# A decoder layer's RWKV mixer in units of two head pairs by 256 tokens, not one pair by 512

## The chip, the cores and the metric

The kernel runs on one core of a Trainium2 chip. The metric is the time of one execution in microseconds (us); "before" is the median of three runs. The profile is of one more execution of the same kernel.

## What is computed

One layer of a decoder for 1024 prompt tokens and 8 sample tokens (1032 columns, held as three pieces of 344 or as four of 256, the last with the 8 samples on top): a SwiGLU FFN, a token mixer, cross-attention into 256 memory tokens, a second FFN, each with a residual and a layer norm. The mixer is what the change touches:

```python
proj = h @ P['w_in']                       # RWKV columns, LRU columns, gates
...
def step(S, inp):                          # per head: 64 x 64 state S
    r_t, w_t, k_t, v_t, kk_t, a_t = inp
    sa = jnp.einsum('bhvk,bhk->bhv', S, -kk_t)
    S = S * w_t[:, :, None, :] + sa[..., None] * (kk_t * a_t)[:, :, None, :] + v_t[..., None] * k_t[:, :, None, :]
    y = jnp.einsum('bhvk,bhk->bhv', S, r_t)
    return S, y
...
_, hs = lax.associative_scan(_lin_combine, (a_t, b_t), axis=1)      # RG-LRU
merged = gates[:, :, 0] * rwkv_out + gates[:, :, 1] * lru_out
out = merged @ P['w_mix_out']
...
mk = (mem_prompt @ xa_wk[l]) ; mv = (mem_prompt @ xa_wv[l])         # attention's memory
```

There are 16 heads of 64 channels, held as 8 pairs of 128 partitions. The 8 samples take one step of the same recurrence from a given state.

## The kernel before

Matrix products keep fp32 accuracy by three products each (`mm3`, L125 to L127): the weight's high part times the input's high and low part (`wh` with HH, HL), and its low part `wl` with HH. Below such a product is called a gemm, and a gemm matmul of the mixer has 344 columns. A weight arrives in halves of 128x512: `split_half` loads one into a tile `raw` (L94, a DMA that SP issues), ScalarE (ACT) rounds it to `wh` (L99), VectorE (DVE) makes `wl` from `raw` and `wh` (L100), and only then is `raw` free. How many `raw` tiles and pairs of `wh`, `wl` there are is set by `more_weights`; in the mixer there is one `raw` and three of the others.

The mixer's recurrence goes in chunks of 64 tokens, in 16 units. Unit t is pair p = t//2 and half u = t%2: one pair by 512 tokens, 8 chunks. For a unit there is `stage` (elementwise work and the matrices within a chunk, SC, BK, AR, QZ), `inverse` (the inverse of the chunks' triangular matrices, on DVE and through DRAM, which ends with the PE group `m<-TB` at L932), and `chain` (the walk over the chunks). A chunk of `chain` has three dependent hops: `ch<-QZ,SC` (L1051), copied by DVE to `wsb` (L1053); `ch<-wsb,TT` (L1057), copied to QZ by DVE (L1063) for one head and by ACT for the other; `y<-QZ,BK` (L1067), scaled by DVE into the next chunk's QZ (L549). After four chunks a `post` makes the group norm and the gates of 256 tokens. `branch` is the RG-LRU; `samples_a`, `samples_b`, `samples_c` are the samples of a pair. In `samples_b` each row of a small DRAM tile T is broadcast by DMA into a tile `row` (L1115) and DVE combines it with the states. `project`, called by `gemms`, does the input projection.

The loop over the units runs `rounds(26, streams, ...)`: in each of 26 rounds each stream (the chain of the unit before, the inverse, the stage of the next unit, branches, samples, gemms) takes its share of steps. That is the order of the program; a list scheduler then fixes, when the kernel is built, the order on every engine, and on the chip each engine runs its list from top to bottom. A DMA that SP is to issue stands in SP's list too.

In the last two units the gemms are those of `out_proj`, the product with w_mix. Behind the loop, `actx.close()` frees the mixer's buffers, `more_weights(S, ctx, 2, 1)` makes it three `raw` and four hl tiles, and the tail begins: the last chain, `out_last` (the last part of w_mix's product, onto `acc<-HD`, the residual), the layer norm, and `memory_kv`, which multiplies the memory by wk and wv: 32 halves, 384 matmuls (`kv<-memh,wh` and the like). Then come the queries and the first scores of attention, `s<-kvh,qh`.

Of the kernel before, what the change touches and what calls it, by code (L numbers as in the profile page):

```python
# [10 lines left out]
F32 = mybir.dt.float32  # L11
# [523 lines left out]

LATE = ("ev", "ref", "dend", "scl", "sm", "wsb", "sf", "ysb", "gsq", "ivc", "bv", "lm")


def mixer(octx, S, I, O, MG, HD, pre):
# [13 lines left out]
    with ExitStack() as ctx:  # L553
# [98 lines left out]
        def gemms(p):  # L652

            for q, xs, early in ((p + 1, tiles(p + 1)[:3], True), (p, tiles(p)[3 + (p == 0):], False)):
                if q < S.npairs:
                    for x in xs:
                        yield from project(q, *x, load_split(S, I["w_in"][x[0]]), CH3, psg, t1)
                    ends(q, early)


        with ExitStack() as c2:
# [78 lines left out]
        stages = itertools.cycle([st0] * 2 + [actx.enter_context(tc.tile_pool(name="msa", bufs=4))] * 4)  # L740
# [6 lines left out]
        def inv_norm(sq, ob, c, op, q, r, tag):  # L747
# [9 lines left out]
            yield  # L757
# [7 lines left out]
        def stage(p, n, P):  # L765

            col = lambda t: t[:, p:p + 1]
            c0, w = NCW[n]
            st = next(stages)
# [9 lines left out]
            for i in range(3):  # L779
                x = tmp("x%d" % i)[:, :w]  # L780
                mt = 8 * i + p
                ACT(x, R[:, i, 1:1 + w], scale=omu[:, mt:mt + 1])
                STT(x[:, 0:256], R[:, i, 0:256], mu[:, mt:mt + 1], x[:, 0:256], ALU.mult, ALU.add)
# [13 lines left out]
            if n == 3:  # L797
                P.sv = t1.tile([128, 6, 8], F32, tag="sv", name="sv", bufs=2)
                P.sg = t1.tile([128, 3, 8], F32, tag="sg", name="sg", bufs=2)
# [13 lines left out]
            bv = tmp("bv", 264, 6)[:, :w]  # L813
            TTo(bv, xv, pb, ALU.mult)
# [4 lines left out]
            ref, dend = P.ref, P.dend  # L819
# [6 lines left out]
            if n == 3:  # L826
# [3 lines left out]
                nc.vector.tensor_copy(out=P.sg[:, 0, :], in_=bv[:, 256:264])  # L830
# [15 lines left out]
            SC, BK = [], []  # L846
            QZ = st.tile([128, 4, 2, 64], F32, tag="QZ", name="QZ")
# [6 lines left out]
            for h in range(2):  # L854
                sc = st.tile([128, 4, 128], F32, tag="SC%d" % h, name="SC%d" % h)
                TTo(sc, q[h], mask.unsqueeze(1).to_broadcast([128, 4, 128]), ALU.mult)
                for b in range(2):
                    r0 = 64 * h + 32 * b
                    nc.sync.dma_start(out=P.D1[n // 2][b, h, 4 * (n % 2):4 * (n % 2) + 4].rearrange("c s t -> s c t"),
                                      in_=sc[r0:r0 + 32, :, 32 * b:32 * b + 32])  # L860
                ACT(P.L21[n // 2][64 * h:64 * h + 32, 4 * (n % 2):4 * (n % 2) + 4, :], sc[64 * h:64 * h + 32, :, 32:64])
# [20 lines left out]
            P.AR.append(AR)  # L882
            P.SC.append(SC)
            P.BK.append(BK)
            P.QZ.append(QZ)

        def inverse(p, u, P):

            TT = TTs[u]

            iv = ta.tile([128, 32, 32], F32, tag="iv", name="iv")
            for q in range(4):
                nc.sync.dma_start(out=iv[32 * q:32 * q + 32], in_=P.D1[u].rearrange("b h c s t -> (b h c) s t"))
# [27 lines left out]
            for h in range(2):  # L921
                B0 = slice(64 * h, 64 * h + 32)
                nc.vector.transpose(out=TN[B0], in_=TT[B0, :, 0:32])
                for c in range(0, 8, 2):
                    nc.tensor.matmul(q[half[h], c // 2, :], P.L21[u][B0, c:c + 2, :].rearrange("p c t -> p (c t)"),
# [12 lines left out]
            for n in (2 * u, 2 * u + 1):  # L938
                for h in range(2):
                    ACT(P.SC[n][h][half[h], :, 0:64], P.AR[n][half[h], :, 0, :])  # L940

        def branch(p, n, P):

            col = lambda t: t[:, p:p + 1]
            c0, w = NCW[n]
            if n == 0:
                P.wg = ta.tile([128, 2, 128], F32, tag="wg", name="wg")
# [17 lines left out]
            gr, gi, th = tmp("gr")[:, :w], tmp("gi")[:, :w], tmp("th")[:, :w]  # L965
# [14 lines left out]
            hs = tmp("lm", 264, 3)  # L980
# [3 lines left out]
            P.hl = tmp("hl", 9, 2)  # L984
# [19 lines left out]

        def post(p, n, P, Y):

            col = lambda t: t[:, p:p + 1]
            c0 = NCW[n][0]
# [3 lines left out]
            ACT(ysb, Y[:, 0:256])  # L1012
            yield
            q = Y[:, 256:512]
            nc.tensor.matmul(q, ones64, ysb, start=True, stop=True)
            TTo(ysb, ysb, q, ALU.subtract)
            ACT(sq, ysb, AF.Square)
            yield
            rs = yield from inv_norm(sq, ob64, GN_EPS, ALU.add, Y[:, 0:4], lambda: Y[:, 256:512], "ivc")
# [9 lines left out]
            if p < S.npairs - 1:  # L1029
                nc.sync.dma_start(out=MG[p, :, 256 * n:256 * n + 256], in_=ysb)  # L1030
            else:
                direct(p, 256 * n, 256, ysb)

        def chain(p, u, P):

            col = lambda t: t[:, p:p + 1]
            TT = TTs[u]
            U8 = slice(8 * u, 8 * u + 8)
            scl = tmp("scl", 8, 2)
            TTo(scl, P.dend[:, U8], P.ref[:, 8 * u + 1:8 * u + 9], ALU.add)  # L1040
            ACT(scl, scl, AF.Exp, scale=-C0)
            for c in range(8 * u, 8 * u + 8):
                n, cc = divmod(c, 4)
                c8 = c - 8 * u
                QZ, SC, BK, AR = P.QZ[n], P.SC[n], P.BK[n], P.AR[n]
                if cc == 0:
                    Y = pst("y", 512, 2)
                    Yc = Y[:, 0:256].rearrange("p (c t) -> p c t", t=64)
                pw, pz = psc(64), Y[:, 256 + 64 * cc:320 + 64 * cc]
                for h in range(2):  # L1050
                    nc.tensor.matmul(pw[half[h]], SC[h][:, cc, 0:64], QZ[:, cc, h, :], start=True, stop=True)  # L1051
                wsb = tmp("wsb", 64, 2)
                nc.vector.tensor_copy(out=wsb, in_=pw)  # L1053
                yield
                pu = psc(64)
                for h in range(2):
                    nc.tensor.matmul(pu[half[h]], TT[half[h], c8, :], wsb[half[h]], start=True, stop=True)  # L1057
                for h in range(2):
                    nc.tensor.matmul(Yc[half[h], cc, :], QZ[half[h], cc, h, :], AR[half[h], cc, 1, :], start=True,
                                     stop=False)  # L1060
                for h in range(2):
                    nc.tensor.matmul(pz[half[h]], ident[half[h], half[h]], QZ[half[h], cc, h, :], start=False, stop=False)
                nc.vector.tensor_copy(out=QZ[half[0], cc, 0, :], in_=pu[half[0]])  # L1063
                ACT(QZ[half[1], cc, 1, :], pu[half[1]])
                yield
                for h in range(2):
                    nc.tensor.matmul(pz[half[h]], BK[h][:, cc, :], QZ[:, cc, h, :], start=False, stop=False)  # L1067
                for h in range(2):
                    nc.tensor.matmul(Yc[half[h], cc, :], QZ[:, cc, h, :], SC[h][:, cc, 64:128], start=False,
                                     stop=True)  # L1070
                if c == 15:
                    sf = tmp("sf", 64)
                dst = [sf[half[h]] if c == 15 else P.QZ[(c + 1) // 4][half[h], (c + 1) % 4, h, :] for h in range(2)]
                for h in range(2):
                    TSC(dst[h], pz[half[h]], scl[half[h], c8:c8 + 1], None, ALU.mult, None)
                yield
                if cc == 3:
                    yield post(p, n, P, Y), 8
            if u == 1:
                nc.sync.dma_start(out=O["prwkv"][p], in_=sf)  # L1080

        def samples_a(p, P):
# [3 lines left out]
            v = tmp("v8", 8, 2, t1)  # L1086
# [11 lines left out]
            s = tmp("sT", 128, 1, t1)[0:40]  # L1098
# [4 lines left out]
        def samples_b(p, P):  # L1103

            y, T3 = tmp("y8", 8, 2, t1), P.T3
            P.y8 = y
            sv = P.sv
            b8 = lambda t: t.unsqueeze(2).to_broadcast([128, 8, 64])
            s_, t_ = (ta.tile([128, 8, 64], F32, tag=x, name=x) for x in ("ws", "wt"))
            nc.sync.dma_start(out=s_, in_=I["srwkv"][p].rearrange("p (b k) -> p b k", k=64))  # L1110

            def row(j):
                t = ta.tile([128, 8, 64], F32, tag="row", name="row", bufs=1)
                for h in range(2):
                    nc.sync.dma_start(out=t[half[h]], in_=T3[8 * j:8 * j + 8, 64 * h:64 * h + 64].unsqueeze(  # L1115
                        0).to_broadcast([64, 8, 64]))
                return t

            yield
            TTo(t_, s_, row(3), ALU.mult)  # L1120
# [534 lines left out]
```

## Time and profile before

| | us |
|---|---|
| runs | 3216.65, 3216.25, 3211.92; median 3216.25 |
| profiled execution | 3214.64, of which span 3212.9 |
| FFN 1 | 0 to about 740 |
| first projections and unit 0's stage and inverse | to 934.5 (end of the first inverse) |
| mixer's rounds | to 2019.9 (start of the last matmul of the last inverse) |
| tail of the mixer, memory's keys and values, queries | to 2181.3 (first scores) |
| attention and FFN 2 | to 3212.9 |

A PE record is a matmul pass: a matmul of 64 columns in fp32 leaves two. "idle before" is the time in which an engine stood still just before a group, with the one that released it. Records such as `x4` are several of one kind in a row. The granted clock is 1.00 when TensorE runs at full speed.

### The profile page before, as it was taken

To read this page: it belongs to the slowest core of one execution; us is meant where nothing else is said; L and a number is where in the kernel's file an instruction comes from. 1 tells how busy PE (TensorE), PEld (TensorE's weight loads), DVE (VectorE), ACT (ScalarE), POOL (GpSimd) and SP (SyncE) were. 2 spreads that over 40 slices of the span, in tenths; PEclk is the share of its full clock that TensorE was granted. 3 is DMA by queue.
4 is the path that set the end of the run, shared out by engine and by line. 5 is a ranking of instruction groups with operands and counts; after the bars stand their busy time and mean duration, and the time that the engine had idled before them with its cause. 6 is when DMAs were issued, how large, how long until landed. Compare 5 with 4: busy or idle time off the path is not lost. (4 is left out here: it accounts for less than half of the span.)

```text
span 3212.9 us, 63092 instructions
## 1 busy us (share of the span) xinstructions
PE 3068.3 (95%) x23312; PEld 2857.1 (89%) x23312; DVE 2247.5 (70%) x6072; ACT 1458.9 (45%) x3259; POOL 565.0 (18%) x526
## 2 busy tenths in 40 slices
PE   8999999999899999999999999889897999999997
PEld 8999999998798888887888878778887999999997
DVE  7666665574578887777888777666667666666556
ACT  5333352125546565656566665364235433334112
POOL 2222200132000101011010010250005322220111
PEclk9999999999999999999999989999999999999998
DMA  4222253314644444444444454654433222225321
GB/s 139 80 78 80 80 159 106 112 47 140 198 122 128 120 119 120 119 131 116 129 119 125 119 145 121 187 161 134 144 117 117 78 80 80 80 80 158 106 86 53
DMA packets 361078, 370.73 MB, mean 115 GB/s; under 512 B 141728, under 2 KB 259904, under 8 KB 360768
## 3 DMA queue, kind: packets, MB, share of 16 engines
q1 hardware_dynamic: 360768, 366.69, 38.3%
q8 instruction: 183, 3.00, 0.4%
q14 instruction: 127, 1.04, 0.1%
HBM read 269.42 MB, written 97.37 MB: 114 GB/s over the span
## 5 line engine op out<-in xcount | busy, mean ns | idle before, releaser
L125 PE MATMUL ps<-HH,wh 128*128 128x258 f32 (+1 forms) x2384 | 719.6, 302 | 17.2 <-ACT HH L508 7.5
L126 PE MATMUL ps<-HL,wh 128*128 128x258 f32 (+1 forms) x2384 | 717.8, 301 | 0.1
L127 PE MATMUL ps<-HH,wl 128*128 128x258 f32 (+1 forms) x2384 | 716.8, 301 | 0.0
L125 PE MATMUL g<-HH,wh 128*128 128x344 f32 (+2 forms) x1840 | 632.3, 344 | 18.5 <-ACT wh L99 5.9
L126 PE MATMUL g<-HL,wh 128*128 128x344 f32 (+2 forms) x1840 | 592.6, 323 | 0.9 <-POOL HL L215 0.8
L127 PE MATMUL g<-HH,wl 128*128 128x344 f32 (+2 forms) x1840 | 589.6, 323 | 0.5 <-DVE hl L991 0.2
L125 PEld LDWEIGHTS ps<-HH,wh 128*128 128x128 f32 x2384 | 452.4, 190 | 19.3 <-ACT HH L508 7.5
L126 PEld LDWEIGHTS ps<-HL,wh 128*128 128x128 f32 x2384 | 452.0, 190 | 0.6 <-DVE HL L509 0.5
L127 PEld LDWEIGHTS ps<-HH,wl 128*128 128x128 f32 x2384 | 451.3, 189 | 0.0
L125 PEld LDWEIGHTS g<-HH,wh 128*128 128x128 f32 x1840 | 354.4, 193 | 45.7 <-ACT wh L99 8.8
L126 PEld LDWEIGHTS g<-HL,wh 128*128 128x128 f32 x1840 | 355.3, 193 | 5.9 <-POOL HL L215 1.5
L127 PEld LDWEIGHTS g<-HH,wl 128*128 128x128 f32 x1840 | 353.0, 192 | 6.6 <-DVE wl L100 1.8
L228 ACT ACTIVATE wh<-raw 128x512 fp32r<-128x512 f32 x280 | 176.5, 631 | 322.0 <-PE ps L126 264.9
L334 POOL TENSOR_TENSOR raw<-raw 128x512 f32<-128x512 f32 x160 | 214.1, 1338 | 566.4 <-DVE wl L229 359.7
L229 DVE TENSOR_TENSOR wl<-raw,wh 128x512 fp32r<-128x512 f32 x280 | 205.3, 734 | 139.0 <-ACT wh L228 132.1
L100 DVE TENSOR_TENSOR wl<-raw,wh 128x512 fp32r<-128x512 f32 x301 | 218.6, 733 | 97.7 <-ACT wh L99 96.1
L99 ACT ACTIVATE wh<-raw 128x512 fp32r<-128x512 f32 x301 | 185.1, 626 | 217.8 <-PE ps L126 75.2
L442 DVE SCALAR_TENSOR_TENSOR acc<-ps,acc 128x344 f32<-128x344 f32 x336 | 168.4, 512 | 141.2 <-PE ps L127 140.6
L546 DVE TENSOR_TENSOR pr<-tq,iv 128x2 f32<-128x2 f32 (+30 forms) x496 | 162.3, 327 | 4.9 <-DVE iv L894 0.3
L551 ACT ACTIVATE ev<-g 128x344 f32<-128x344 f32 x192 | 87.3, 455 | 98.0 <-PE g L127 84.7
L754 POOL TENSOR_TENSOR ivc<-ivc,mhalf 128x4 f32<-128x4 f32 x32 | 34.9, 1090 | 526.4 <-DVE ivc L549 478.9
L551 ACT ACT_TABLE_LOAD x96 | 123.2, 1283 | 5.8 <-DMA raw<-in_w_in_dram 2.0
(417 smaller groups left out, 6570.5 us busy)
## 6 DMA issues: line engine op xcount, KB each, us to landing
raw<-in_wi_dram SPq DMA_DIRECT2D x176, 256.0 KB, 2.9
raw<-in_w_in_dram SPq DMA_DIRECT2D x116, 256.0 KB, 3.0
GD<-ev SPq DMA_DIRECT2D x168, 172.0 KB, 2.0
raw<-in_wo_dram SPq DMA_DIRECT2D x104, 256.0 KB, 3.1
raw<-HID SPq DMA_DIRECT2D x88, 258.0 KB, 3.2
HID<-g SPq DMA_DIRECT2D x80, 258.0 KB, 2.2
row<-T SPq DMA_DIRECT2D x80, 128.0 KB, 3.0
GD<-t SPq DMA_DIRECT2D x24, 344.0 KB, 4.0
```

The lines of the kernel that those rows point to most:

```text
L99: nc.scalar.activation(out=hi, in_=raw, func=AF.Identity)
L100: nc.vector.tensor_tensor(out=lo, in0=raw, in1=hi.bitcast(F32), op=ALU.subtract)
L125: nc.tensor.matmul(ps, wh, xh, start=first, stop=False)
L126: nc.tensor.matmul(ps, wh, xl, start=False, stop=False)
L127: nc.tensor.matmul(ps, wl, xh, start=False, stop=last)
L228: nc.scalar.activation(out=hi, in_=x, func=AF.Identity)
L229: nc.vector.tensor_tensor(out=lo, in0=x, in1=hi.bitcast(F32), op=ALU.subtract)
L334: pool_tt = lambda o, a, b, op: nc.gpsimd.tensor_tensor(out=o, in0=a, in1=b, op=op)
L442: nc.vector.scalar_tensor_tensor(out=a, in0=q, scalar=0.5 / ALPHA, in1=a, op0=ALU.mult, op1=ALU.add)
L546: TTo = lambda o, a, b, op: nc.vector.tensor_tensor(out=o, in0=a, in1=b, op=op)
L551: ACT = lambda o, a, f=AF.Identity, **kw: nc.scalar.activation(out=o, in_=a, func=f, **kw)
L754: nc.gpsimd.tensor_tensor(out=v, in0=v, in1=mhalf[:, 0:4], op=ALU.pow)
```

## The change

A unit is a group of two pairs by 256 tokens: group g = t//4, quarter n = t%4, still 16 units, each 4 chunks of 4 heads. So there are 64 chunk steps, each with the matmuls of two steps before. The three products of a step share one PSUM tile `ch`; the copies to `wsb` (now 128x128) and QZ (64x2x64) serve both pairs, and the scaling is a `TENSOR_TENSOR` with a broadcast factor. The loop has 13 rounds a unit. The gemms are one continuous stream, of which unit t takes FILL[t] steps; unit 0's stage is woven with 42 of them, and `rest` projects four tiles ahead of the rounds where it did two. Two posts follow a unit, one behind the other. `samples_b` runs both pairs of a group, one after the other, each in two halves of four samples, and loads its rows into the work tile `wt` itself, so that a load waits for the last use of `wt` and the next DVE step for the load. `out_proj` leaves out two pairs for all eight m, and `out_last` adds both for all of them. In the tail `more_weights(S, ctx, 2, 1)` is gone: the one `raw` and three hl tiles of the mixer stay.

```diff
 # rest(), ahead of the mixer's rounds
-                for x in tiles(0)[2:4]:
-                    yield from project(0, *x, load_split(S, I["w_in"][x[0]]), CH3, psl, lp)
-                ends(0, True)
+                for p, i in ((0, 2), (1, 0), (1, 1), (1, 2)):
+                    x = tiles(p)[i]
+                    yield from project(p, *x, load_split(S, I["w_in"][x[0]]), CH3, psl, lp)
...
-            weave((low_out(), 29), (rest(), 17))
+            weave((low_out(), 29), (rest(), 49))
...
 # post
-            ACT(ysb, Y[:, 0:256])
+            ACT(ysb, Y)
...
-            if p < S.npairs - 1:
+            if p < S.npairs - 2:
                 nc.sync.dma_start(out=MG[p, :, 256 * n:256 * n + 256], in_=ysb)
...
 # chain
-            for c in range(8 * u, 8 * u + 8):
...
-                pw, pz = psc(64), Y[:, 256 + 64 * cc:320 + 64 * cc]
+            for c in range(4):
...
+                ch = psc(384).rearrange("p (x i t) -> p x i t", i=2, t=64)
+                pw, pu, pz = (ch[:, x] for x in range(3))
+                for i, h in both:
+                    nc.tensor.matmul(pw[half[h], i], SC[i][h][:, c, 0:64], QZ[:, i, c, h, :], start=i == 0, stop=i == 1)
+                wsb = tmp("wsb", 128, 2).rearrange("p (i t) -> p i t", t=64)
+                nc.vector.tensor_copy(out=wsb, in_=pw)
+                yield
+                for i, h in both:
+                    nc.tensor.matmul(pu[half[h], i], TT[half[h], 4 * i + c, :], wsb[half[h], i], start=i == 0, stop=i == 1)
+                for i, h in both:
+                    nc.tensor.matmul(Yc[half[h], i, c, :], QZ[half[h], i, c, h, :], AR[i][half[h], c, 1, :], start=i == 0,
+                                     stop=False)
+                for i, h in both:
+                    nc.tensor.matmul(pz[half[h], i], ident[half[h], half[h]], QZ[half[h], i, c, h, :], start=i == 0,
+                                     stop=False)
+                nc.vector.tensor_copy(out=QZ[half[0], :, c, 0, :], in_=pu[half[0]])
+                ACT(QZ[half[1], :, c, 1, :], pu[half[1]])
+                yield
+                for i, h in both:
+                    nc.tensor.matmul(pz[half[h], i], BK[i][h][:, c, :], QZ[:, i, c, h, :], start=False, stop=i == 1)
+                for i, h in both:
+                    nc.tensor.matmul(Yc[half[h], i, c, :], QZ[:, i, c, h, :], SC[i][h][:, c, 64:128], start=False,
+                                     stop=i == 1)
...
                 for h in range(2):
-                    TSC(dst[h], pz[half[h]], scl[half[h], c8:c8 + 1], None, ALU.mult, None)
-                yield
-                if cc == 3:
-                    yield post(p, n, P, Y), 8
+                    TTo(dst[h], pz[half[h]], scl[half[h], :, c:c + 1].to_broadcast([64, 2, 64]), ALU.mult)
...
+            yield itertools.chain(*(post(U.p0 + i, n, Y[:, 256 * i:256 * i + 256]) for i in range(2))), 14
 # samples_b
-            s_, t_ = (ta.tile([128, 8, 64], F32, tag=x, name=x) for x in ("ws", "wt"))
...
-                t = ta.tile([128, 8, 64], F32, tag="row", name="row", bufs=1)
...
-            TTo(t_, s_, row(3), ALU.mult)
...
+            for b0 in (0, 4):
+                B = slice(b0, b0 + 4)
+                s_, t_ = (ta.tile([128, 4, 64], F32, tag=x, name=x) for x in ("ws", "wt"))
...
+                row(3)
+                yield
+                TTo(t_, s_, t_, ALU.mult)
...
+                row(1)
+                yield
+                TTo(s_, s_, t_, ALU.mult)
+                row(4)
...
 # out_last
-                for i in ((0, 1) if m < 4 else (1,)):
+                for i in range(2):
...
 # the mixer's loop
-            s = [(chain((t - 1) // 2, (t - 1) % 2, Ps[(t - 1) // 2]), 27)] if t else []
-            s.append((inverse(p, u, Ps[p]), 52))
+            g, n = divmod(t, 4)
+            s = [(chain(units[t - 1], units[t]), 13)] if t else []
+            s.append((inverse(units[t]), 52))
...
-            if u == 1:
-                s.append((samples_b(p, Ps[p]), 6))
...
-                s.append((g if whole else part(g, 42), 73 if t == 0 else 49 if t == nu - 3 else 43))
-            if t == nu - 2:
-                s.append((out_proj(range(4), KT - 2, range(KT - 2), ("ev", "ws", "wt", "ev", "row")), 46))
-            if t == nu - 1:
-                s.append((out_proj(range(4, 8), KT - 1, (KT - 2,)), 37))
-            rounds(26, s, late_steps, t < nu - 2)
+            if n == 3:
+                s.append((pairs_of(samples_b, g), 21))
+            elif n == 1 and g:
+                s.append((pairs_of(samples_c, g - 1), 10))
+            s.append((part(fill, FILL[t]) if t < nu - 1 else fill, FILL[t]))
+            rounds(13, s, late_steps, t < nu - 1)
...
         S.norms = Norms(S, octx)
-        more_weights(S, ctx, 2, 1)
-        wp = ctx.enter_context(tc.tile_pool(name="wmix", bufs=3))
+        wp = ctx.enter_context(tc.tile_pool(name="wmix", bufs=4))
...
-        weave((chain(S.npairs - 1, 1, Ps[-1]), 45), (early(), 43), (part(mem, 35), 20))
+        weave((chain(units[-1], None), 45), (early(), 43), (part(mem, 35), 20))
```

How many there are on each engine, before and after, by the built program: PE 20828 and 20840, DVE 5946 and 5769, ACT 3225 and 3156 (100 and 92 table loads among them), POOL 531 and 531, SP 2029 and 2118 (row loads 80 and 160). Between the first matmul of `stage` and the last of `chain`, PE goes from other work to a gemm 501 times before and 356 times after, the other work falls into 1298 groups of one kind before and 887 after, and 4348 and 4032 gemm matmuls stand there, the difference ahead and behind. Groups of 24 or more matmuls without a gemm between them number 8 with 274 matmuls before, 14 with 573 after; of at least 38 matmuls, 4 and 8.

PE's list in a unit before (g is a gemm's PSUM tile, `ch` and `y` belong to the chain):

```order
L1057 MATMUL ch<-wsb,TT_8799 64x64 x2
L1059 MATMUL y<-AR,QZ 64x64 x2
L1062 MATMUL y<-QZ,ident 64x64 x2
L125 MATMUL g<-HH,wh 128x344
L126 MATMUL g<-HL,wh 128x344
L127 MATMUL g<-HH,wl 128x344
L125 MATMUL g<-HH,wh 128x344
L126 MATMUL g<-HL,wh 128x344
L127 MATMUL g<-HH,wl 128x344
L1067 MATMUL y<-QZ,BK_17805 64x64
L1067 MATMUL y<-QZ,BK_17841 64x64
L1069 MATMUL y<-SC_17717,QZ 64x64
```

The second and third hop of a chunk have six gemm matmuls between them. At the place that answers to it, PE's list after:

```order
L1077 MATMUL ch<-wsb,TT_8800 64x64 x4
L1082 MATMUL ch<-QZ,ident 64x64 x4
L1090 MATMUL y<-SC_16315,QZ 64x64
L1088 MATMUL ch<-QZ,BK_16335 64x64
L1088 MATMUL ch<-QZ,BK_16388 64x64
L1088 MATMUL ch<-QZ,BK_16751 64x64
L1088 MATMUL ch<-QZ,BK_16753 64x64
L1090 MATMUL y<-SC_16320,QZ 64x64
L1090 MATMUL y<-SC_16680,QZ 64x64
L1090 MATMUL y<-SC_16685,QZ 64x64
L1079 MATMUL y<-AR,QZ 64x64
L1072 MATMUL ch<-QZ,SC_16315 64x64
```

The hops of one step, with four matmuls each, stand one behind the other, and the next step's first hop follows at once; 47 gemm matmuls stand just ahead.

SP's list in the tail before (`row<-T` are the rows of `samples_b`, `raw<-in_wk_dram` the memory's weights, `f<-FD` what `out_proj` has stored):

```order
L1115 DMA row<-T_24714 64x8x64
L94 DMA raw<-in_w_mix_dram 128x4x128
L1187 DMA FD<-ev 128x344
L94 DMA raw<-in_w_mix_dram 128x4x128
L1187 DMA FD<-ev 128x344
L94 DMA raw<-in_w_mix_dram 128x4x128
L1193 DMA acc<-HD 128x8x256
L1187 DMA FD<-ev 128x344
L1202 DMA f<-FD 128x256
L1305 DMA mi<-in_memT_dram 128x256 x2
L1202 DMA f<-FD 128x256
L94 DMA raw<-in_wk_dram 128x512
```

The same place after:

```order
L1142 DMA wt<-T_24151 64x4x64 x2
L94 DMA raw<-in_wk_dram 128x512
L1031 DMA tg<-GD_8811 128x2x256
L1163 DMA out_srwkv_dram<-ws 128x256
L1142 DMA wt<-T_24151 64x4x64 x2
L94 DMA raw<-in_wk_dram 128x512
L1225 DMA acc<-HD 128x8x256 x2
L1234 DMA f<-FD 128x256 x2
L1357 DMA KD<-mo 128x256
L1358 DMA out_mk_dram<-mo 128x256
L94 DMA raw<-in_wk_dram 128x512
```

The load of the residual now stands behind ten row loads (`wt<-T`, pairs of DMAs) that follow the last inverse's loads `TB<-D`, where before one pair did, and the fourth load of wk stands behind it. On PE the first `kv` matmul has moved behind the last chunk step and both posts; before, they were mixed. The list of `kv` matmuls after ends with 180 in a row that only some layer norm matmuls interrupt, 46 matmuls of queries, and then the first scores.

More of the change, by code (lines that the diff above doesn't have):

```diff
@@ L650, in ends, with gemms @@
                 nc.sync.dma_start(out=O["conv"][:, p, :], in_=GD[p][:, GL, NP - 3:NT])
[L652 to L658, printed above, removed]
+        ready = set()
+        def gemms():
+            for g in range(S.npairs // 2):
+                ps_ = (2 * g, 2 * g + 1)
+                for xs, early in (((0, 1, 2), True), ((3, 4, 5), False), ((6,), False)):
+                    if g or not early:
+                        for p in ps_:
+                            for x in (tiles(p)[i] for i in xs):
+                                yield from project(p, *x, load_split(S, I["w_in"][x[0]]), CH3, psg, t1)
+                                ready.add((p, x[1]))
+                            if 6 not in xs:
+                                ends(p, early)
+            ready.add("h")
+            yield from out_proj()
         with ExitStack() as c2:
@@ L755, in inv_norm @@
             ACT(sq.rearrange("p (g c) -> p g c", c=64), v.unsqueeze(2).to_broadcast([128, 4, 64]))
-            yield
-            yield
+            for _ in range(wait):
+                yield
             r = r()
@@ L763, in mixer, with stage @@
         c3 = lambda t: t[:, 0:256].rearrange("p (c t) -> p c t", t=64)
-        def stage(p, n, P):
+        def stage(U, i):
+            p, n, P, st = U.p0 + i, U.n, Ps[U.p0 + i], U.st
             col = lambda t: t[:, p:p + 1]
             c0, w = NCW[n]
-            st = next(stages)
+            assert all((p, j) in ready for j in range(3))
             R = ta.tile([128, 3, 265], F32, tag="R", name="R", bufs=1)
@@ L1063, in chain @@
[L1063 to L1070, printed above, removed]
@@ new lines, in chain @@
+                yield
[4 more added lines that the diff above has]
+                                     stop=i == 1)
+                if n == 3 and c == 3:
+                    sf = tmp("sf", 128).rearrange("p (i t) -> p i t", t=64)
+                    dst = [sf[half[h]] for h in range(2)]
+                elif c == 3:
+                    dst = [V.QZ[half[h], :, 0, h, :] for h in range(2)]
+                else:
+                    dst = [QZ[half[h], :, c + 1, h, :] for h in range(2)]
@@ L1103, in samples_b @@
         def samples_b(p, P):
[L1105 removed]
+            y, T3 = tmp("y8", 8, 4, t1), P.T3
             P.y8 = y
             sv = P.sv
[L1108 to L1117 removed]
@@ L1210, in mixer @@
         Ps = []
+        units = []
         def stage_unit(t):
[L1213 to L1221 removed]
@@ new lines, in stage_unit, with branches @@
+            U.st, bufs = next(stages)
+            U.QZ = U.st.tile([128, 2, 4, 2, 64], F32, tag="QZ", name="QZ", bufs=bufs)
+            U.L21 = ta.tile([128, 8, 32], F32, tag="L21", name="L21", bufs=2)
+            U.D1 = dr.tile([2, 2, 8, 32, 32], F32, tag="D1", name="D1")
+            units.append(U)
+            for i in range(2):
+                yield from stage(U, i)
+            for i in range(2 if n == 3 else 0):
+                yield from samples_a(U.p0 + i, Ps[U.p0 + i])
+        def branches(ts):
+            for t in ts:
+                for i in range(2):
+                    p = 2 * (t // 4) + i
+                    yield from branch(p, t % 4, Ps[p])
```

249 lines of the change are left out of this document (121 added, 128 removed).

## The prediction

> **What bounds the kernel now.** I read the page's busy times first, then the windows by unit, then the timeline of PE in a quiet place and in a bad one, and last the tail by its tiles. Everything is set against the profiled execution, 3214.64 us, which lies 1.6 us under the median of the runs shown; its span is 3212.9, so 1.7 us lie around it.
>
> ```profile
> PE 3068.3 (95%) x23312; PEld 2857.1 (89%) x23312; DVE 2247.5 (70%) x6072; ACT 1458.9 (45%) x3259; POOL 565.0 (18%) x526
> PE   8999999999899999999999999889897999999997
> ```
>
> PE bounds nearly everything; the only soft stretch beside the start is slices 26 to 31, the mixer's end and its tail. By windows (first column the window, then its length; next PE, PEld, DVE, ACT, POOL busy, the granted clock, DMA share, GB/s) four units, a part of the last of them, and the two halves of the tail:
>
> ```profile
> 1001.60:1070.50 68.90, 67.58 (x573) 58.24 (x572) 57.90 (x207) 47.55 (x108) 6.87 (x7) 1.00 0.44 126
> 1070.50:1142.10 71.60, 68.73 (x573) 60.04 (x572) 57.22 (x192) 37.01 (x88) 9.62 (x8) 0.98 0.45 121
> 1142.10:1214.10 72.00, 69.00 (x573) 58.68 (x572) 56.16 (x203) 48.20 (x106) 6.34 (x7) 1.00 0.43 123
> 1214.10:1292.20 78.10, 75.12 (x572) 62.83 (x571) 61.22 (x202) 39.48 (x94) 7.96 (x8) 0.91 0.44 122
> 1220.00:1240.00 20.00, 19.44 (x118) 14.61 (x118) 12.78 (x56) 7.49 (x15) 4.24 (x4) 0.68 0.39 106
> 2019.90:2100.00 80.10, 71.36 (x547) 61.17 (x545) 53.13 (x143) 30.59 (x79) 30.83 (x37) 0.91 0.64 193
> 2100.00:2181.00 81.00, 66.20 (x488) 63.44 (x487) 57.24 (x113) 50.24 (x124) 43.61 (x52) 0.92 0.48 148
> ```
>
> A unit takes about 71 us, in which PE stands still for 1.3 to 3 us; DVE is busy for 57. The fourth unit has as many matmuls and takes 78.1, because the clock is 0.91, and 0.68 near its start. In the tail PE is idle for 9 and 15 us in 80. So the mixer's price is PE's own issue, and the tail's price is what its loads and chain allow. I take the two apart.
>
> **Fewer interruptions of the gemms.** What one costs, from PE's timeline in a unit (start, us, operation):
>
> ```profile
> 1003.34 0.32 PE L126 MATMUL g<-HL,wh 128*128 128x344 f32 x1
> 1003.50 0.32 PE L127 MATMUL g<-HH,wl 128*128 128x344 f32 x1
> 1003.75 0.34 PE L1051 MATMUL ch<-QZ,SC 128*64 128x64 f32 x4
> 1004.02 0.42 PE L125 MATMUL g<-HH,wh 128*128 128x344 f32 x1
> 1004.28 0.32 PE L126 MATMUL g<-HL,wh 128*128 128x344 f32 x1
> 1004.43 0.32 PE L127 MATMUL g<-HH,wl 128*128 128x344 f32 x1
> ...
> 1214.11 0.91 PE L932 MATMUL m<-TB,M 64*64 64x32 f32 x16
> 1214.95 0.43 PE L125 MATMUL g<-HH,wh 128*128 128x344 f32 x1
> ```
>
> Gemm matmuls follow each other every 0.16 us. Three of them after 1003.50 would end the row at a start of 1003.97; it is 1004.43, so a group of four small records cost 0.46. The long group at 1214.11 gives 0.84/16 = 0.053 a record, 0.21 for four, and the interruption itself is left with 0.25. The lower end is what the first gemm's own row shows, 0.42 against 0.32, so 0.10. I take 0.22, near the upper row, since that holds both edges. PE's list has 145 fewer (501 to 356): 145 x 0.22 = -32 us, between -15 and -36. All of it lies on PE, which has no slack in these units.
>
> **Joint groups.** The step's matmuls are as many as before, but there are 411 fewer groups (1298 to 887). L1051's four records took 0.27 to the next start, 0.06 over 4 x 0.053; that end holds a part of the interruption already counted, the other end is nothing. I take 0.03: -12 us, between 0 and -25. The joint copies save DVE 64 `wsb` copies, as many of QZ, and 120 scalings; ACT loses 64 copies:
>
> ```profile
> L1053 DVE COPY wsb<-ch 128x64 f32<-128x64 f32 x120 | 26.7, 223 | 32.4 <-PE ch L1051 29.7
> L1051 PE MATMUL ch<-QZ,SC 128*64 128x64 f32 x480 | 50.1, 253 | 4.4 <-DVE QZ L549 3.9 <-DVE tq L902 0.4
> L1057 PE MATMUL ch<-wsb,TT 64*64 64x64 f32 x480 | 41.1, 246 | 2.8 <-DVE wsb L1053 2.8
> L1067 PE MATMUL y<-QZ,BK 128*64 128x64 f32 x480 | 56.8, 252 | 2.7 <-DVE QZ L1063 1.4 <-ACT QZ L551 1.1
> ```
>
> I cost that at nothing: in these groups of all rounds PE waited 4.4 + 2.8 + 2.7 = 9.9 us for the chain (the third number after the bars), so DVE's work is hidden by gemms. With half as many steps the waits could fall by 5 us at most, unless the hops, now closer to each other, meet nothing to hide them.
>
> **Groups without a gemm.** That is the open term. Of the fourth unit's bad place the timeline shows:
>
> ```profile
> 1217.13 0.29 PE L1097 MATMUL m<-ident,sv 128*40 128x128 f32 x1 [0.97 <-ACT TT L551]
> 1224.60 0.48 PE L1051 MATMUL ch<-QZ,SC 128*64 128x64 f32 x2 [0.56 <-DVE QZ L549]
> 1225.63 1.22 PE L968 MATMUL m<-xc,wg 128*128 128x256 f32 x2
> 1230.82 0.66 PE L125 MATMUL g<-HH,wh 128*128 128x344 f32 x1
> ```
>
> No gemm stands between the first and the last of these rows, and the matmuls take about twice their time (a gemm 0.66 against 0.32). The unit is 78.1 - 70.8 = 7.3 us longer than the mean of the other three. PE's list has four such long groups before and eight after. At 7.3 each that is +29. Against it, the 40 matmuls of an old group held a little over two chunk steps of two heads, and a step now serves four, so the new groups may pass without the clock falling; if the old four go and the new cost nothing, -29. The row nearest is the 9.9 us of chain waits, of which half goes: I take -5.
> [...]
>
> **The samples' rows.** 80 more row loads, and each DVE step now waits for a load that waits for the step before. One such trip in the tail, issue to use:
>
> ```profile
> 2021.68 0.61 SPq L1115 DMA_DIRECT2D row<-T  x1
> 2025.87 0.67 DVE L546 TENSOR_TENSOR wt<-ws,row 128x512 f32<-128x512 f32 x1
> ```
>
> 4.2 us; with a DVE operation of half the 0.67 the 20 steps of a group come to some 91 us, more than a unit. DVE's list lets them run on into the next unit, and at the trace's durations the other work between two of them mostly comes to more than 5 us, so most trips are covered; a step that comes late holds up what stands behind it on DVE, and PE feels that only through a chain copy. SP's queue is passed too: a `raw` load behind a waiting row load comes later. Bounds: nothing, and 25 us, if each of the 40 added steps comes 0.6 us late; I take +3. That the 344-column gemms number 316 fewer in the rounds is no gain; they stand ahead and behind. Unit 0's stage among gemms is counted at nothing, since PE's slices there read 9.
>
> **The tail.** With one `raw`, a load, ACT's `wh` and DVE's `wl` follow each other. Such a cycle in the mixer, where `raw` is single, and loads of the tail with three:
>
> ```profile
> 1159.37 0.33 SPq L94 DMA_DIRECT2D raw<-in_w_in_dram  x1
> 1162.85 0.63 ACT L99 ACTIVATE wh<-raw 128x512 fp32r<-128x512 f32 x1 [0.24 <-DMA raw<-in_w_in_dram]
> 1163.51 0.69 DVE L100 TENSOR_TENSOR wl<-raw,wh 128x512 fp32r<-128x512 f32 x1 [0.20 <-ACT wh L99]
> 1164.23 0.33 SPq L94 DMA_DIRECT2D raw<-in_w_in_dram  x1
> ...
> 2130.01 4.82 SPq L94 DMA_DIRECT2D raw<-in_wv_dram  x4
> 2136.88 5.69 SPq L94 DMA_DIRECT2D raw<-in_wv_dram  x4
> ```
>
> One half in 4.86 us, against eight in 12.6. Before, with E = 2019.9 the last inverse's end:
>
> ```profile
> L932 PE MATMUL m<-TB,M x256: 218/220/242, 934.5 to 2019.9; 64*64 64x32 f32 x128
> 2030.72 0.49 SPq L1193 DMA_DIRECT2D acc<-HD  x1
> L126 PE MATMUL kv<-meml,wh x64: 278/283/467, 2046.0 to 2114.9; 128*128 128x256 f32 x64
> L126 PE MATMUL kv<-wl,memh x64: 276/280/391, 2117.3 to 2148.3; 128*128 128x256 f32 x64
> 2178.65 0.28 PE L127 MATMUL g<-HH,wl 128*128 128x256 f32 x1
> 2178.77 0.28 PE L125 MATMUL g<-HH,wh 128*128 128x264 f32 x1
> 2181.32 0.34 PE L125 MATMUL s<-kvh,qh 128*128 128x256 f32 x1
> ```
>
> The residual's load goes at E + 10.8, `kv` runs from E + 26 to E + 128.4, and the first scores stand at E + 161.4. After, ten row steps follow the last inverse on SP; at 4.2 to 4.9 us (a trip, and two DVE operations of half the old 0.67) they end at E + 42 to E + 49, say E + 45. The fourth of 32 halves is loaded only then, so 29 cycles follow. At 4.86 that is 141 us; the layer norms now share ACT and DVE with the conversions, so I take 5.1: 148 us. Behind the last half stand some 12 `kv` matmuls and 46 of the queries, 58 x 0.12 = 7 us. Scores at E + 45 + 148 + 7 = E + 200, +38 us. What else the tail has (the added 48 matmuls of `out_last`, the layer norms) lies in that stretch, on engines that wait for loads. Ends: rows at E + 30, cycles of 4.5 with the landing at once, E + 168, +7; cycles of 5.5 and E + 49, E + 216, +55; 60 with a late `post`.
>
> **Sum.** -32 - 12 - 5 + 3 + 38 = -8 us: 3214.64 - 8 = 3206.6, say 3207.
>
> **Rivals.**
> 1. The tail is not bound by `raw`: the scheduler's order has loads ahead that I take as late, or rows go faster. For it: before, PE was the busier engine in the tail, 71 of 80 us. Against it: `kv` stands behind the chain on PE, and three hl tiles hold at most three halves. Price: the tail's +7 in place of +38: 3176.
> 2. Slower by the tail's `raw`: each half takes 5.5 us as ACT and DVE serve the layer norms between, rows at E + 49, and the gain in the mixer is the lower end of the interruptions (-15 in place of -32). Price: 55 - 15 - 12 - 5 + 3 = +26: 3241. It decides from the point where 29 cycles and the rows cost more than the interruptions give, at 5.4 us a cycle with my other terms.
> 3. Slower by the clock: all eight long groups cost 7.3 us as the one before. +29 in place of -5 gives +26: 3241. For it: clock 0.68 while PE was busy all the time. Against it: half the hops.
> 4. The mixer gains more: interruptions at 0.25, groups at 0.06, and the long groups free: -36 - 25 - 29 + 3 + 38 = -49: 3166.
>
> **How the numbers follow.** About 0.2% (6.4 us) is what a measurement of this kernel can tell from no change. My sum, within some 15 us (3192 to 3222): 0.38, of which 0.19 faster, 0.12 the same, 0.07 slower. Rival 1: 0.20. Rival 2: 0.20, of which 0.02 the same. Rival 3: 0.14. Rival 4: 0.08. So faster 0.47, same 0.14, slower 0.39. The range takes in rivals 1 to 3 with their near ends, and leaves out rival 4 and the joint case of 2 and 3: 3168 to 3252.
>
> **What would show it.** Right: units at about 68 us between ends of the inverse with fewer PE edges; in the tail `raw` loads 5 us apart until the last `wv`, the residual's load some 45 us after the last inverse, scores near E + 200. Wrong: units of 71 us or more with the clock below 0.95 in many (rival 3), or a tail of 170 us (rival 1). A row load that holds up the chain on DVE would show as `wt` waiting for DMA in units 3, 7, 11 and 15.

## The result, and the profile after

The changed kernel takes 3326.45 us (3322.83 to 3330.36), the kernel before in the same job 3215.95: a ratio of 1.0346, 95% interval 1.0329 to 1.0364, some 110 us slower. The forecast was 3207. From the page after, span, busy times and the granted clock by slice:

```profile
span 3321.4 us, 63119 instructions
PE 3080.6 (93%) x23324; PEld 2896.4 (87%) x23324; DVE 2199.0 (66%) x5895; ACT 1433.5 (43%) x3190; POOL 554.5 (17%) x526
PEclk9999999999999999999998888768999999999998
```

The clock row reads 8 or less in slices 22 to 28, from the mixer's last third to the end of the tail. By the same marks in both traces (us; gemm matmuls of the stretch, and the difference at equal work, at 0.157 us a matmul of 344 columns and 0.12 of 256, their spacing at a clock of 1.00):

| stretch | before | after | gemm matmuls | at equal work |
|---|---|---|---|---|
| to the first matmul of `stage` | 849.5 | 863.0 | +142 | -9 |
| to the end of the first inverse | 85.8 | 97.4 | +65 | +1 |
| mixer, to the end of the last inverse | 1084.7 | 1097.7 | -223 | +48 |
| tail, to the first scores | 161.4 | 217.8 | -90 | +67 |
| to FFN 2 | 278.9 | 294.1 | +118 | +1 |
| FFN 2 | 744.1 | 742.8 | | -1 |

So two stretches lose, and the change's own gain is not to be seen in the sum. It is to be seen in single units. Windows of units 3, 5, 6 and 14 after (length; PE, PEld, DVE, ACT, POOL busy; clock; DMA share; GB/s):

```profile
1165.30:1248.80 83.50, 72.67 (x576) 63.51 (x576) 60.81 (x204) 43.87 (x100) 5.40 (x6) 0.89 0.47 131
1320.10:1384.80 64.70, 62.60 (x574) 56.70 (x574) 48.87 (x182) 39.98 (x97) 9.31 (x8) 1.00 0.38 106
1384.80:1464.70 79.90, 71.80 (x569) 63.52 (x569) 56.16 (x184) 44.46 (x89) 6.09 (x6) 0.87 0.42 114
1976.70:2057.60 80.90, 61.41 (x477) 52.15 (x477) 56.63 (x187) 38.92 (x77) 3.10 (x3) 0.83 0.46 125
```

Units 0, 1, 5 and 9, the four fastest, take 65.2, 66.0, 64.7 and 65.5 us at a clock of 0.97 in unit 0 and 1.00 in the others, where before the same ones took 67.0, 68.9, 69.6 and 69.8. The eleven others take 68 to 85. From the first matmul of `stage` to the last inverse the clock is below full for 198 us, before 72 (below, the time below full clock in the mixer is always counted so). In the mixer itself, stretches of more than 5 us from one gemm matmul to the next come to 142 us, before 62. One of them, in unit 3, on PE:

```profile
1183.49 0.32 PE L127 MATMUL g<-HH,wl 128*128 128x344 f32 x1
...
1184.68 0.45 PE L1077 MATMUL ch<-wsb,TT 64*64 64x64 f32 x8
...
1186.05 0.45 PE L1088 MATMUL ch<-QZ,BK 128*64 128x64 f32 x8
...
1190.90 0.33 PE L1079 MATMUL y<-AR,QZ 64*64 64x64 f32 x2 [0.63 <-DVE QZ L548]
1195.37 1.22 PE L985 MATMUL m<-xc,wg 128*128 128x264 f32 x2 [4.14 <-DVE tq L917]
1196.70 0.66 PE L125 MATMUL g<-HH,wh 128*128 128x344 f32 x1
```

Two chunk steps run hop after hop, then PE waits 4.14 us for DVE. DVE's stage work comes late since DVE itself stood still before, for a hop that stands behind a row of gemms on PE:

```profile
1184.34 0.29 DVE L1074 COPY wsb<-ch 128x128 f32<-128x128 f32 x1 [4.45 <-PE ch L1072]
```

What SP issues meanwhile (rows left out between):

```profile
1164.74 0.43 SPq L94 DMA_DIRECT2D raw<-in_w_in_dram  x1
...
1175.64 1.27 SPq L1142 DMA_DIRECT2D wt<-T  x2
...
1180.64 1.26 SPq L1142 DMA_DIRECT2D wt<-T  x2
...
1189.58 1.25 SPq L1142 DMA_DIRECT2D wt<-T  x2
...
1192.02 0.43 SPq L94 DMA_DIRECT2D raw<-in_w_in_dram  x1
```

And what ACT makes of that load:

```profile
1196.01 0.63 ACT L99 ACTIVATE wh<-raw 128x512 fp32r<-128x512 f32 x1 [5.36 <-DMA raw<-in_w_in_dram]
```

The `raw` tile was free at 1174.1, when `wl` of the load of 1164.74 was made; the next weight load goes out 18 us later, behind row loads that wait for their DVE step and a load of the states. ACT stands still for 5.36 us until it has landed, and the first gemm on PE, at 1196.70, starts as soon as `wh` is made. So here the gemms have no weights. And when they come back the clock is down, 0.50 from 1192.2 to 1199.0. What that is worth a gemm shows in unit 4, where the clock fell among gemms (0.50 from 1243.5 to 1253.5, PE busy for all 10 us); before and after its return:

```profile
1250.33 0.49 PE L127 MATMUL g<-HH,wl 128*128 128x344 f32 x1
1250.62 0.49 PE L125 MATMUL g<-HH,wh 128*128 128x344 f32 x1
...
1253.88 0.32 PE L125 MATMUL g<-HH,wh 128*128 128x344 f32 x1
1254.04 0.32 PE L126 MATMUL g<-HL,wh 128*128 128x344 f32 x1
```

0.29 us a gemm matmul, then 0.16. In the clock's records the low stretches of the mixer last from 3.4 to 20.5 us, most of them (18 of 20) 3.4, 6.8, 10.2 or 13.7, each at 0.50.

The tail after (loads of weights, first and last `kv`, first scores; "first to last" in us):

```profile
L947 PE MATMUL m<-TB,M x256: 219/219/313, 959.7 to 2058.2; 64*64 64x32 f32 x128
L94 SPq DMA_DIRECT2D raw<-in_wk_dram x16: 332/334/537, 2084.1 to 2184.6; - x16
L94 SPq DMA_DIRECT2D raw<-in_wv_dram x16: 327/332/406, 2188.9 to 2261.2; - x16
L125 PE MATMUL kv<-memh,wh x64: 276/280/580, 2105.1 to 2190.6; 128*128 128x256 f32 x64
L126 PE MATMUL kv<-wl,memh x64: 281/415/583, 2196.2 to 2266.4; 128*128 128x256 f32 x64
L125 PE MATMUL s<-kvh,qh x32: 276/282/579, 2276.0 to 2384.3; 128*128 128x256 f32 x32
2220.00:2276.00 56.00, 40.52 (x169) 33.53 (x169) 9.75 (x15) 10.62 (x22) 0.00 (x0) 0.59 0.30 94
```

One half of wv in 4.82 us, as in the mixer before (4.86), and in the last window PE has only 169 matmuls in 56 us, DVE and ACT some 10 us of work each: the loads bound it.

### The profile page after: what moved, and what is told of

Read it like the earlier page. It is cut to its first block, busy times and chain, and to the rows that moved or that the text cites. A ratio compares the mean times of both kernels' runs of the same rounds, so it can differ in the third digit from the quotient of the medians.

```text
span 3321.4 us, 63119 instructions
## 1 busy us (share of the span) xinstructions
PE 3080.6 (93%) x23324; PEld 2896.4 (87%) x23324; DVE 2199.0 (66%) x5895; ACT 1433.5 (43%) x3190; POOL 554.5 (17%) x526
## 5 line engine op out<-in xcount | busy, mean ns | idle before, releaser
L126 PE MATMUL g<-HL,wh 128*128 128x344 f32 (+2 forms) x1840 | 602.2, 328 | 1.3 <-DVE HL L548 1.3
L127 PE MATMUL g<-HH,wl 128*128 128x344 f32 (+2 forms) x1840 | 598.8, 327 | 4.8 <-DVE wl L100 4.8
L125 PEld LDWEIGHTS g<-HH,wh 128*128 128x128 f32 x1840 | 361.7, 197 | 39.8 <-ACT wh L99 9.7
L127 PEld LDWEIGHTS g<-HH,wl 128*128 128x128 f32 x1840 | 360.4, 196 | 12.2 <-DVE wl L100 7.9
L917 DVE TENSOR_REDUCE tq<-pr 128x1 f32<-128x2 f32 (+30 forms) x496 | 121.6, 245 | 2.9
L374 ACT ACTIVATE g<-g 128x258 f32<-128x258 f32 x160 | 67.1, 419 | 112.9 <-DVE g L333 112.0
```

Source lines behind the costliest of these rows:

```text
L125: nc.tensor.matmul(ps, wh, xh, start=first, stop=False)
L126: nc.tensor.matmul(ps, wh, xl, start=False, stop=False)
L127: nc.tensor.matmul(ps, wl, xh, start=False, stop=last)
L917: nc.vector.tensor_reduce(out=tq[:, 0:m, i], in_=pv, axis=mybir.AxisListType.X, op=ALU.add)
```

## The experiments

"b" is the kernel before with an edit, "a" the changed one. Ratios are to the kernel before on the same chip; a difference of 0.001 is 3.2 us.

**1. One raw tile in the tail of the kernel before (b_raw1).**

```diff
-        more_weights(S, ctx, 2, 1)
```

> The kernel before with one line out: the tail's call of more_weights, so one raw tile and three hl tiles serve w_mix, wk, wv and the queries there, as after. In the traces of both kernels the tail (last inverse to first scores) went from 161.4 to 217.8 us. Theory R, the single raw tile makes the tail load-bound: 29 to 32 cycles of about 5 us, a tail of 190 to 205 us, the whole 3250 +- 10. Rival S, the late start does it (rows of the samples ahead of the residual's load, keys and values only behind the chain), the raw tile little: below 3228, tail below 175 us.

3274.87 us, 1.0201 (1.0176 to 1.0225), +65 us.

```profile
L94 SPq DMA_DIRECT2D raw<-in_wk_dram x16: 327/333/384, 2049.9 to 2143.3; - x16
L94 SPq DMA_DIRECT2D raw<-in_wv_dram x16: 327/332/398, 2150.0 to 2215.6; - x16
L125 PE MATMUL s<-kvh,qh x20: 276/283/388, 2231.2 to 2296.9; 128*128 128x256 f32 x20
```

The tail is 211.7 us, 50 more than before, with the loads about as far apart as after the change, though keys and values start 36 us behind the last inverse and not 47. Theory R holds and its price was too low; nearly the whole of the tail's loss of 56 us is this one line. Leaving it out buys nothing here: the buffers of the joint units take its room.

**2. The number of rounds and the queue of the rows (b_r13, a_r26, a_poolq, a_r26q).**

```diff
-            rounds(26, s, ...)          # b_r13; a_r26 the other way
+            rounds(13, s, ...)
...
-                        nc.sync.dma_start(out=t_[half[h]], in_=T3[...
+                        nc.gpsimd.dma_start(out=t_[half[h]], in_=T3[...          # a_poolq
```

> The kernel before with 13 rounds a unit in place of 26, all else as it was. Theory L, the coarser rounds lump the order, so that PE has long stretches without a gemm and the clock falls: at least 20 us slower, 3236 or more, and more than 110 us below full clock in the mixer (72 before, 198 after the change). Rival Q, the samples' rows and stores on SP's list hold up the weight loads: within 10 us of 3216, as the samples are those of before.

> The changed kernel with 26 rounds a unit in place of 13. Theory L: at least 20 us faster than 3326, 3306 or less, with less time below full clock. Rival Q: within 10 us of 3326. If the joint steps themselves make the lumps, also within 10 us.

> The changed kernel with the row loads of samples_b (160 of them) issued by GpSimd, not SP. Theory Q: weight loads no longer stand behind row loads that wait, so units 3, 7 and 11 lose most of their 10 to 15 us and the residual's load comes earlier: 3280 to 3300. Rival L: within 10 us of 3326. If rows on GpSimd hold up its pow operations, slower than 3326.

> The changed kernel with 26 rounds a unit and with the row loads issued by GpSimd. Alone these gave 17 and 24 us. Two separate causes in the mixer: about 40 us together, 3286 +- 8. One cause met twice: 3300 or more. In either case the tail stays at 215 to 235 us, since it has one raw tile.

b_r13: 3249.82, 1.0113 (1.0092 to 1.0135), but with 68 us below full clock in the mixer, not 110: time was lost, not by the mechanism named. a_r26: 3309.43, 1.0300 (1.0276 to 1.0324), 15 us less than the change; a_poolq: 3302.48, 1.0280 (1.0257 to 1.0304), 21 us less; a_r26q, both: 3292.51, 1.0225 (1.0177 to 1.0273), 39 us less. That fits two causes that add (15 and 21 make 36), but the interval of a_r26q is 15 us to each side. In the traces' mixers alone, at nearly equal work, it is 22, 15 and 32 us. In the built order the groups of 24 or more matmuls without a gemm (to the last inverse) go from 13 to 9, 9 and 3.

**3. The rows on GpSimd in the kernel before (b_poolq), and with 13 rounds (b_r13q).** The edit is the same.

> The kernel before with the row loads issued by GpSimd: whether they cost only where there are twice as many and in a chain. Theory Q: before has 5 steps a unit where the change has 20, so 0 to 6 us of gain, 3208 to 3216. If the gain is 15 us or more, the rows held up SP before as well, and the change only kept that.

> The kernel before with 13 rounds a unit and the row loads on GpSimd. 13 rounds alone cost 37 us, rows on GpSimd alone gave 61. In the built order of PE it has one group of 24 or more matmuls without a gemm, as the kernel with the rows on GpSimd has (before 7 up to the last inverse, 13 with the change). If the two causes are separate: 3190 to 3205, units some 2 us longer than with 26 rounds though the clock hardly falls. If the loss of 13 rounds is only long groups and clock: 3155 to 3170.

b_poolq: 3161.02, 0.9813 (0.9771 to 0.9855): 60 us faster than the kernel before, the second case of the expectation at four times its bound. Units 2 to 11 all take 68.0 to 69.5 us. Units 4 and 6, which took 78.1 and 69.3 before, and GpSimd's waits ahead of row loads (us in total, times, longest):

```profile
1207.90:1277.10 69.20, 68.08 (x574) 58.47 (x573) 59.57 (x201) 37.95 (x93) 15.65 (x18) 1.00 0.48 131
1346.00:1415.40 69.40, 68.00 (x573) 58.52 (x573) 59.98 (x203) 38.59 (x94) 15.67 (x18) 1.00 0.47 132
POOL row L1115 <- DVE wt L546: 83.5, 14, 10.1
POOL row L1115 <- DVE pr L546: 65.9, 12, 7.0
```

On GpSimd, which is busy for 15.65 of the 69.20 us of unit 4, the row loads can wait. 13.7 us are left below full clock in the mixer; the long groups went from 7 to 1. But the edit changes the built order as well as the queue. The slow place of unit 4 before, and the same place in b_poolq (rows left out between):

```profile
1218.18 0.28 SPq L1101 DMA_DIRECT2D T<-sT  x1
1218.89 0.42 SPq L94 DMA_DIRECT2D raw<-in_w_in_dram  x1
1226.18 0.42 ACT L551 ACTIVATE s<-ivs 128x256 f32<-128x256 f32 x1 [3.37 <-POOL ivs L754]
1226.34 1.31 SPq L1115 DMA_DIRECT2D row<-T  x2
1228.77 0.61 ACT L99 ACTIVATE wh<-raw 128x512 fp32r<-128x512 f32 x1
...
1213.20 0.28 SPq L1101 DMA_DIRECT2D T<-sT  x1
1218.21 0.43 SPq L94 DMA_DIRECT2D raw<-in_w_in_dram  x1
1222.17 0.61 ACT L99 ACTIVATE wh<-raw 128x512 fp32r<-128x512 f32 x1
```

Before, the weight load of 1218.89 goes out 20 us after `raw` was free (1199.0), and what stands ahead of it is a store of `samples_a`, not a row load. It had landed at 1221.65, but ACT rounds it only at 1228.77, since ACT's list has work ahead of it that waits for GpSimd. In b_poolq the load is just as late (`raw` was free at 1197.5), and no place without gemms comes of it: ACT rounds it 4 us after its issue, where it was 10 us before, and the gemms still in stock are spread over the time until then. So the queue of the rows alone doesn't explain this place. The same shows in counts: `raw` stands free for more than 10 us ahead of 11 loads of the mixer before, of 6 in b_poolq and of 12 after the change, and a stretch of more than 5 us without a gemm lies beside 3, none and all 12 of them. A late load cost time where the order had spent the stock of gemms in one row: in unit 3 after, 44 gemm matmuls in a row and then 102 records of other work. How much of the 60 us is the queue and how much the order was not told apart. b_r13q: 3227.23, 1.0030 (1.0016 to 1.0044): 70 us slower than b_poolq, more than either case, at 34 us below full clock. There every unit is 2 to 6 us longer, and the time is in the small groups (93 a unit for 85). With units of one pair 13 rounds put two hops in a round, which the joint units don't have, so this run doesn't price the change's 13 rounds; a_r26 does.

**4. Room for a second raw tile, and gemms for the last units (a_r26q_raw2, a_f2).**

```diff
+        S.rawseq = itertools.cycle([ctx.enter_context(tc.tile_pool(name="xwraw", bufs=1)), S.wraw])
-            bv = tmp("bv", 256, 8)
+            bv = tmp("bv", 256, 6)
...
-FILL = [42] * 11 + [37] * 5
+FILL = [42] * 3 + [40] * 13          # a_f2, on top
```

> The kernel of the run beside it with a second raw tile in the tail (a tile pool of one buffer; six bv buffers in place of eight make the room). Theory R: the loads of wk and wv overlap with the conversions, the tail loses 30 to 55 of the 56 us that it gained by the change, 3230 to 3260. Rival S: under 15 us, as the start at some 47 us behind the last inverse stays.

> The changed kernel with 26 rounds, rows on GpSimd and a second raw tile (3238), and FILL = [42] * 3 + [40] * 13: units 2 to 9 give 12 gemm matmuls each to the later ones. If the last units wait for want of gemms: 5 to 20 us faster, 3218 to 3233. If groups without a gemm decide (198 matmuls in them in place of 125): 3240 to 3255.

a_r26q_raw2: 3237.62, 1.0050 (1.0028 to 1.0073), 56 us less than without the second tile.

```profile
L94 SPq DMA_DIRECT2D raw<-in_wv_dram x16: 327/333/402, 2125.2 to 2169.2; - x16
L125 PE MATMUL s<-kvh,qh x32: 276/283/387, 2184.9 to 2292.9; 128*128 128x256 f32 x32
```

One half of wv in 2.9 us, and a tail of 167.1 us. a_f2: 3206.24, 0.9991 (0.9971 to 1.0010), 19 us less again by the ratios: its mixer takes 1033.5 us where the run without took 1058.1, with 16 gemm matmuls fewer. Without it units 13 and 14, with 179 and 250, took 82 us each. The result fits the first case, units 2 to 9 with more gemms than their chain needed and the last ones with too few; unit 13 still spends 34 of its 77 us below full clock.

**5. Without the samples' state update (a_nosb, b_nosb, a_nosb_r26_raw2).** States are loaded and stored back; rows and VectorE operations are left out.

> The changed kernel with the samples' state update left out of samples_b: states loaded and stored back, no rows, no VectorE operations on them. With the rows on GpSimd it gained 24 us. If rows on SP's list are the samples' whole part of the loss: 3295 to 3310. If their operations on VectorE and their waits also count: below 3285. The residual's load no longer stands behind rows, so the tail should lose at most 30 us more, or nothing if it is bound by the one raw tile alone.

> The kernel before with the samples' state update left out of samples_b, as in the changed kernel's run (3262, 65 us less than with it). If SP's list is the whole cost of the rows in the kernel before: 3153 to 3165, as with the rows on GpSimd. If the operations on VectorE also count: 3130 to 3150. If before lost little to the samples: 3190 or more.

> The changed kernel without the samples' state update, with 26 rounds and a second raw tile. Theory U, the joint unit itself is the faster one by some 3 us a unit, as the undisturbed units were: 10 to 45 us faster than the run beside it. Theory V, the joint steps pack the chain's hops and starve the last units of gemms: slower than the run beside it by 5 us or more, with units 12 to 14 far below full clock and units 0 to 9 at 65 us.

a_nosb: 3261.51, 1.0132 (1.0106 to 1.0157), 69 us less, of which 55 lie in the mixer; units 3, 7 and 11 take 68, 69 and 62 us where they took 83, 78 and 85. The tail, with the first `kv` at 30 us behind the last inverse in place of 47, is still 210.4 us: the late start counts for 7 us. b_nosb: 3153.94, 0.9830 (0.9806 to 0.9854), 55 us less than before, no more than b_poolq gave: there the operations on VectorE cost nothing that shows. So the samples' update costs 69 us after and 55 before, and the change makes it dearer by some 14 us only, with about 13 to each side. Set against each other, a_nosb and b_nosb have no row loads at all, and still the mixer of the changed kernel loses: 1042.4 us with 3555 gemm matmuls against 1037.0 with 3783, 41 us more at equal work, where it was 48 with the samples. What the mixer lost by the change is for the most part not the rows. a_nosb_r26_raw2: 3159.69, 0.9843 (0.9813 to 0.9873), against which b_nosb's interval overlaps. With the samples, the rounds and the tail out of the way the whole is neither faster nor slower. Its units 0 to 9 take 64 to 72 us, on the mean 67.4 where b_nosb's take 68.4; its last three take 64, 80 and 72 with 55 us below full clock, and 567 gemm matmuls where b_nosb's have 753 in the same time. At equal work the mixer alone is 16 us longer (1013.4 us with 3531 gemm matmuls against 1037.0 with 3783). So theory V's loss is there; the time outside the mixer, the tiles projected ahead above all, makes up for it in the sum.

**6. One part alone, and the best version (b_front, b_allq, b_frontallq).**

```diff
-                for x in tiles(0)[2:4]:          # b_front: rest; gemms and unit 0's 73 steps to match
+                for x in tiles(0)[2:6]:
```

> The kernel before with one part of the change alone: rest projects four tiles of pair 0 ahead of the rounds where it did two, the first unit's rounds two fewer. The traces have 148 gemm matmuls more (23 us) ahead of the mixer for 13.8 us of time. If PE's idle time there is filled for good: 3204 to 3212. If the gemms missing later open a gap: 3214 or more.

> The kernel before with all DMAs of samples_a and samples_b on GpSimd, not the row loads alone (3161). In the slow place before, a weight load stood behind a store of samples_a on SP. If such stores still hold up loads: 3145 to 3156. If the row loads were all of it: 3157 to 3165.

> The run beside it, and rest with four tiles as in the run with that part alone, which gave 13 us. Two separate gains: 3140 to 3152. If the first unit's missing gemms now open gaps: 3155 or more.

b_front: 3209.24, 0.9961 (0.9944 to 0.9978), 13 us faster: PE's idle time ahead of the mixer is filled for good. b_allq: 3159.13, 0.9818 (0.9790 to 0.9845), no different from the rows alone. b_frontallq: 3163.13, 0.9829 (0.9804 to 0.9855): the 13 us do not come on top; the mixer has 37.5 us below full clock in place of 30.7, its tail is 4.5 us longer. The kernel before with the rows, or all of the samples' DMAs, on GpSimd is the fastest that ran, some 1.8% under the kernel before and 5% under the changed one.

## Why the prediction was wrong, by its steps

The forecast was 3207 and the time is 3326, 120 us more. In the mixer the sum had 46 us of gain (-32 - 12 - 5 + 3), and the traces show 48 of loss at equal work: that is 94 of the 120. Most of the rest is the size of the tail.

- Groups without a gemm (-5): this step failed. The sum let half of 9.9 us of chain waits go, as the nearest row, and left the clock to rival 3. a_nosb and b_nosb show the step without any rows: where interruptions, joint groups and this term say 49 us less, the mixer takes 41 more. Stretches of more than 5 us without a gemm come to 72 us in eight places in a_nosb, to 12 us in one in b_nosb, and the time below full clock is 140 us against 17; at the 0.50 that the low stretches of the change's own trace show, that is worth some 61 us, an estimate. What the runs show of its causes: the coarse rounds (22 us of the mixer, a_r26) and the shares of gemms in the units (22 us at equal work, a_f2). For the rest of the 90 us between 49 less and 41 more no run shows the cause. Rival 3 named the long groups and the clock, and had 0.14 and a price of 29.
- Fewer interruptions and joint groups (-44 us, 2.9 a unit): reached where a unit is undisturbed, and nowhere else. The means of units 0, 1, 5 and 9 are 65.4 and 68.8, 3.5 less. Only four of fifteen units are so, and they are picked as the fastest. In a_nosb_r26_raw2, where seven of units 0 to 9 run at full clock throughout, the mean of the ten is 1.0 less than in b_nosb; its finer rounds also bring PE back to a gemm more often, 405 times in the trace where a_nosb has 349.
- The samples' rows (+3): the term was the added cost, and that came to some 14 us, within its bound of 25. But the working took each late row as a stall of DVE only. That a `raw` load behind a waiting row load comes later stood in it as a sentence without a price, and unit 3 shows it with 18 us.
- Unit 0 among gemms and the tiles ahead, "no gain": the tiles ahead are worth 9 us in the trace and 13 as a change of their own.
- The tail (+38): the mechanism was right, the size was not, and the start came out near by luck. The residual's load stands at E + 43.0 (E + 45 was forecast), but of the ten row steps four went ahead of E, and the six behind it took 6.7 us each where 4.2 to 4.9 was taken. The fourth half of wk goes out at E + 52.3; the 28 cycles from there to the last half of wv take 5.4 us each (5.1 was taken; one half of wq is among them); the scores come 14.8 us behind that load (12 was taken). So they stand at E + 218, not E + 200; at equal work, since 90 gemms moved behind the scores, the tail lost 67. Of wv a half took 4.82 us. The cycles of wk were longer: a load went out 1.0 us after `raw` was free, on the mean, where wv's went out after 0.1, and from the residual's load to wv's first (2101 to 2190) SP waited with the loads of `f<-FD` for GpSimd's additions (us in total, times, longest):

```profile
SPq L1234 <- POOL acc L1235: 31.4, 29, 5.7
```

What each of these is worth was not tried.

- Rival 2's sum (+26) had the tail near its true price and lost the mixer; rivals 2 and 3 happened together, a case that the range left out.

Not settled: how much of a_r26's 15 us is the finer mixing and how much the scheduler's other order; whether the rows' gain on GpSimd is the queue or the order that the scheduler builds with it; and what makes the part of the mixer's loss that neither the rounds nor the shares of gemms explain. With the rows on GpSimd in both kernels (a_poolq, b_poolq) the mixer of the changed one is 83 us longer at equal work, more than with the rows on SP.

## What to carry to other kernels

Where one queue issues both the loads that feed the bound engine and small DMAs that wait for other engines, look for the loads in that queue's own timeline: in unit 3 after, gemms without weights showed on PE only as 102 records of other work and a wait for DVE (4.14 us). Then look at what the order does with the late load: 21 us late cost no place without gemms in b_poolq, where the gemms in stock were spread, and 18 us cost one after the change, where they had run in one row. A change that makes room for itself by dropping buffers elsewhere is priced at the place that loses them, by the single-buffer cycle times the loads: 32 x some 5 us here was as large as all else. What is gained in an undisturbed unit is multiplied only by the units that stay undisturbed. And a part of both kernels is judged by leaving it out of both: the samples' update cost 69 us after, but 55 of them before as well.

## What was not expected of the hardware

The granted clock fell in places where PE was busy for nearly all of the time by its records: 0.68 over 20 us with PE busy for 19.44 in the kernel before. These were 118 records, 5.9 a us, where an undisturbed unit has 8.3 a us (573 in 68.90); which of the two the clock follows was not tried. The clock stayed down for the first gemms after this place: 0.29 us each from 1231.27, 0.16 from 1233.15. Row loads issued by GpSimd took 0.70 us of that engine each (b_poolq), and its pow operations beside them lost nothing that shows: with 80 of them the kernel was 60 us faster.
